# The last FFN of a streaming-encoder block: group 10 with seven block products, x kept in DRAM until the gated sum, and weights in empty slots

## The chip, the cores and the metric

One NeuronCore of a Trainium2 chip. The metric is the device time of one execution in microseconds, the median of several runs.

## The reference, cut to what matters

The input x has 256 tokens of 2048 float32 values. Three sublayers follow one another, each post-normed and modulated by adaLN rows made of the conditioning vector c:

```
mod = silu(c) @ w_ada + b_ada            # shift, scale, gate for each of the sublayers
x = LN1(alpha*x + 1/2*gate0 * SwiGLU_1(mod0(x)))
x = LN2(alpha*x +     gate1 * W_out[ mLSTM(u) || RG-LRU(u) ])     # u = mod1(x)
x = LN3(alpha*x + 1/2*gate2 * SwiGLU_2(mod2(x)))

_swiglu(u, w13, w2): g, v = split(u @ w13);  return (silu(g) * v) @ w2
```

w13 is 2048 x 11264 and w2 is 5632 x 2048, all float32. The change lies in SwiGLU_2 and in what adds its result to x.

## The kernel before, in words

Float32 products are made on TensorE from float32r halves. Each weight tile (128 x 2048, 1 MB) is loaded from DRAM on SP's queue into a raw tile (`load`, L94), ACT casts it into a high half (L108), and DVE subtracts that from the raw tile into a low half (L110). There are four raw buffers and three pairs of halves. The activations are kept as halves too (`uh`, `ul`). A product of a 512 x 512 weight tile with 128 tokens is `mov_t`: 12 matmuls of 512 columns (four slices, each high x high, high x low, low x high); `mov_w` does both token tiles.

The 5632 hidden columns of the last FFN are 11 blocks of 512 columns. A plain block (`rows_block`, L669) loads four g tiles and four v tiles, splits each, and makes 16 products. Blocks 2 to 9 (`FAST`, L46) go through `fast_block` (L711): for the first half of the contraction the four blocks of weights and four of activations are combined as in Strassen's scheme, and 7 products do the work of 8; with the other half 15 are left of 16. The price is four combinations of whole weight tiles on DVE (L756, L761, L766, L775) and three more splits. The combined activations `ws` are made once, by `sums` (L688), and lie in the tile of x; x is stored to DRAM before (L690). In a fast block four w2 tiles of an earlier pair of blocks run between the products (`x_tile`, L733), and their sum is collected in `yacc`, two of six slots. `turn_one` (L803) transposes the gated activations of the block before into the slots `hth`, `htl`, two for each pair of blocks. A tile of a fast block that is used for long lies in one of two row buffers: `ta` always, `tc_` from block 4 on, when the silu(c) row `scb` has left the other.

After block 9 x is loaded back and scaled by alpha (`restore`, L705), the gate row is made (`gate_rows`), and eight `residual` calls (L330) add gate * yacc to x. Block 10 is a plain block. `closing` (L1026) then multiplies the w2 tiles of blocks 8, 9 and 10: nine in a loop for three of the four column groups, and the last group with the gate folded into the weights; `boundary` does the last layer norm and stores.

The adaLN tiles (1 MB each, a multiply and a reduction on DVE, L210) are scattered between the weight loads: each `load` calls `tick`, which adds a rate to a credit and issues a tile (L206) for every whole unit. 16 of these tiles, the gate's, are left for the last FFN; its credit starts at -2 and grows by 0.5. They use the four raw buffers also, and `scb`. They must be done before the gate row.

The order on each engine is planned by the framework's scheduler when the program is built, from the program's order and a model of the durations; instructions of `T`, `A`, `V`, `G`, `Q` keep their program order among themselves. `fast_block` issues its products on `T`.

Of the kernel before, what the change touches and what calls it, by code (L numbers as in the profile page):

```python
# [41 lines left out]
FFN2_RATE = 0.5  # L42
# [3 lines left out]
FAST = range(2, 10)  # L46


class Held:
# [4 lines left out]
    def __getitem__(self, key):  # L54
        return self.tile[key]
# [3 lines left out]
def block_kernel(ctx: ExitStack, tc: tile.TileContext, a: dict, out: bass.AP):  # L59
# [19 lines left out]
    wide = [False]  # L79
    n_raw = [1]  # L80
# [13 lines left out]
    def load(src, name, into=None, raw=None):  # L94

        tick()
        raw = raw or raw_tile("r" + name)
        queue().dma_start(raw, src)
        return raw, name, into
# [554 lines left out]
    def ffn(s, w13, w2, start, following=None):  # L654
# [8 lines left out]
        b0 = RAMP // 4 if start else 0  # L663
# [5 lines left out]
        def rows_block(b, passed=None):  # L669

            i = 8 * (b - b0)
            if passed:
                pg, pv = passed[0], met(passed, w13[4:8], f"fv{s}")
            else:
                pg = [bank(f"fg{s}{b}{t}") for t in range(NT)]
                for k in range(4):
                    end = mov_w(pg, load_w(w13[i + k], f"fg{s}_{b}{k}"), uh, ul, k * 4, k == 0, k == 3)
                    if k in (1, 2):
                        turn_one(end)
                pv = [bank(f"fv{s}{b}{t}") for t in range(NT)]  # L680
                for k in range(4):
                    mov_w(pv, load_w(w13[i + 4 + k], f"fv{s}_{b}{k}"), uh, ul, k * 4, k == 0, k == 3)
            if 4 * b // GRP not in hts:
                new_h(4 * b // GRP)
            for t in range(NT):
                swiglu(b, t, pg[t], pv[t])

        def sums():  # L688

            nc.gpsimd.dma_start(xd, x.tile)  # L690
            f = raw_tile("sums").rearrange("p (a b) -> p a b", b=P)
            for t in range(NT):
                tk = slice(t * P, (t + 1) * P)
                nc.vector.tensor_add(f[:, 8 * t:8 * t + 8, :], uh[:, 0:8, tk].bitcast(F32), ul[:, 0:8, tk].bitcast(F32))
            a11, a12, a21, a22 = (f[:, 4 * i:4 * i + 4, :] for i in range(4))
            nc.vector.tensor_add(a22, a21, a22)
            nc.vector.tensor_sub(a21, a11, a21)
            nc.vector.tensor_sub(a11, a22, a11)
            nc.vector.tensor_sub(a12, a12, a11)
            both = big.tile([P, 2, KT, P], F32R, tag="x", name="ws")  # L700
            nc.scalar.copy(both[:, 0], f)
            nc.vector.tensor_sub(both[:, 1], f, both[:, 0].bitcast(F32))
            return both[:, 0], both[:, 1]

        def restore():  # L705
            x.tile = tokens("x1")
            for t in range(NT):
                nc.gpsimd.dma_start(x[:, t, :], xd[:, t, :])
            scale_x()

        def fast_block(b, wh, wl):  # L711

            i = 8 * b
            gi = 4 * b // GRP - 1
            s2_, s4_, s3_, s1_ = 0, 4, 8, 12
            p1, p5 = bank(f"fa{b}"), bank(f"fb{b}")
            py = {}

            def part(ps, hl, h, k0, t, first, last):
                return mov_t(ps, hl, *h, k0, t, first, last, T, skip_group_check=not first and ps in (p1, p5))  # L720

            def fresh(k, row=False):
                return load(w13[i + k], f"fw{s}_{b}{k}", None, row_tile(f"fw{b}{k}") if row else None)

            def halves(tile, w=""):
                return split((tile[0], tile[1] + w, None), nc.scalar, nc.vector)

            def kept(ps, tag, w):
                to = sm.tile([P, 512], F32, tag=tag, bufs=2, name=f"{w}{s}{b}")
                nc.scalar.copy(to, ps)  # L730
                return to

            def x_tile(m):  # L733
                n, k = b % 2 * 2 + m // 2, m % 2
                if not k:
                    py[n] = [bank(f"py{gi}_{n}_{t}") for t in range(NT)]
                kg = 2 * gi + k
                end = mov_w(py[n], load_w(w2[kg * 4 + n], f"w2{s}_{kg}_{n}"), *hts[gi], k * 4, not k, k == 1, T)
                if k:
                    c = slice(n * 512, (n + 1) * 512)  # L740
                    for t in range(NT):
                        if gi == 0:
                            evac.append(nc.scalar.copy(yacc[t][:, c], py[n][t]))
                        else:
                            nc.vector.tensor_add(yacc[t][:, c], yacc[t][:, c], py[n][t])
                return end

            u, w = (uh, ul), (wh, wl)
            ta = fresh(0, True)
            end = part(p1, halves(ta), u, 0, 0, True, True)  # L750
            turn_one(end)
            f1 = kept(p1, "u", "fs")
            tc_ = fresh(4, b >= 4)
            end = x_tile(0)
            turn_one(end)
            nc.vector.tensor_sub(ta[0], tc_[0], ta[0])  # L756
            part(p5, halves(ta, "p"), w, s1_, 0, True, True)
            f5 = kept(p5, "gy", "ft")
            td = fresh(5)
            x_tile(1)  # L760
            nc.vector.tensor_sub(ta[0], td[0], ta[0])  # L761
            part(p1, halves(ta, "q"), w, s2_, 0, False, True)
            f2 = kept(p1, "gy", "fv")
            part(p5, halves(td), w, s4_, 0, False, False)
            x_tile(2)
            nc.vector.tensor_sub(tc_[0], td[0], tc_[0])  # L766
            part(p1, halves(tc_, "q"), w, s3_, 0, False, True)
            f3 = kept(p1, "u", "fu")
            p2, p4 = bank(f"fc{b}"), bank(f"fd{b}")
            tb = fresh(1)  # L770
            part(p2, halves(tb), u, 4, 0, True, False)
            g2_ = load_w(w13[i + 2], f"fw{s}_{b}2")
            part(p2, g2_, u, 8, 0, False, False)
            part(p4, g2_, u, 8, 1, True, False)
            nc.vector.tensor_sub(tb[0], tb[0], ta[0])  # L775
            part(p4, halves(tb, "p"), u, 4, 1, False, False)
            g3_ = load_w(w13[i + 3], f"fw{s}_{b}3")
            part(p2, g3_, u, 12, 0, False, True)
            part(p4, g3_, u, 12, 1, False, True)
            nc.vector.tensor_add(f1, f1, p2)  # L780
            nc.scalar.activation(f1, f1, AF.Silu)
            nc.vector.tensor_add(f3, f3, p4)
            nc.scalar.activation(f3, f3, AF.Silu)
            x_tile(3)
            vs = [load_w(w13[i + 4 + k], f"fw{s}_{b}{4 + k}") for k in (2, 3)]
            for t, ps in enumerate((p5, p1)):
                for k in range(2):
                    part(ps, vs[k], u, 8 + 4 * k, t, False, k == 1)
            if 4 * b // GRP not in hts:
                new_h(4 * b // GRP)  # L790
            for t, h, v, ps in ((0, f1, f2, p5), (1, f3, f5, p1)):
                nc.vector.tensor_add(v, v, ps)
                nc.vector.tensor_mul(h, h, v)
                to_turn.append((b, t, h))
# [177 lines left out]
        def g1(gi):  # L972
            grp = groups[gi]
            if start and gi == 2:
# [8 lines left out]
            if start and gi == 3:  # L983
# [3 lines left out]
            for b in range(grp[0] // 4, grp[-1] // 4 + 1):  # L987
                if b or start:
                    rows_block(b)
# [36 lines left out]
        def closing(gi):  # L1026

            kgs = [(kg, hts[kg // 2], kg % 2 * 4) for kg in (2 * gi - 2, 2 * gi - 1, 2 * gi)]
            pss, hls = {}, {}

            def gated(k, into=None):

                tile = load(w2[kgs[k][0] * 4 + 3], f"w2{s}l{k}", into)
                for c in range(0, D, 512):
                    nc.vector.tensor_mul(tile[0][:, c:c + 512], tile[0][:, c:c + 512], gate[:, 1536:])
                hls[k] = split(tile, nc.scalar, nc.vector)

            for i, (n, k) in enumerate(((0, 0), (0, 1), (1, 0), (0, 2), (1, 1), (1, 2), (2, 0), (2, 1), (2, 2))):
                kg, h, k0 = kgs[k]
# [519 lines left out]
```

## Time and profile before

| | us |
|---|---|
| median of 3 runs (1881.72 to 1884.14) | 1883.53 |
| the profiled execution | 1882.46 |
| its span, first to last instruction | 1880.7 |
| TensorE busy in the span | 1861.4 (99%) |
| DVE busy | 1561.3 (83%) |
| ACT busy | 895.1 (48%) |
| GpSimd (POOL) busy | 43.2 (2%) |

The span lacks 1.8 us of the execution's own time. In the rows PE is TensorE, PEld its weight load, DVE VectorE, ACT ScalarE, POOL GpSimd, and SP SyncE, which issues most DMAs; a q behind an engine is its queue. Matmuls are pipelined: a row gives each 0.39 us, while the next begins 0.23 us later, so a busy TensorE can still be held up a little. The last FFN begins near 1148 us and its block 2 at 1242.80 us.

### The profile page before, as it was taken

The page shows a single profiled execution, that of the slowest core. Times are in us where ns is not written, and L with a number is a line of the kernel's source. Part 1 is how long each engine was busy: PE and PEld are TensorE (multiplying, and loading weights), DVE is VectorE, ACT ScalarE, POOL GpSimd, SP SyncE. Part 2 cuts the span into 40 slices and gives each one's busy share as a digit, 9 for nine tenths or more (in the row PEclk, how much of TensorE's full clock was granted, in tenths as well). Part 3 has the DMA queues.
Part 4 walks back from the last instruction along what each step waited for, and adds up shares of the span by engine and source line. Part 5 has one row for each costly group of instructions (what it writes and reads, how often), then busy time and mean ns, then how long its engine had stood idle before and what let it go on. Part 6 is the DMA issues. An engine that isn't in the chain of part 4 may idle for free.

```text
span 1880.7 us, 21240 instructions
## 1 busy us (share of the span) xinstructions
PE 1861.4 (99%) x8495; PEld 1526.0 (81%) x8495; DVE 1561.3 (83%) x1467; ACT 895.1 (48%) x847; POOL 43.2 (2%) x68
## 2 busy tenths in 40 slices
PE   8999999999999999999999999999999999999998
PEld 5788888888888888788888887878778888888886
DVE  6899998887887987889997877789887788778776
ACT  4543444533334335756644356454544455545441
POOL 0000000000000000100000121000000000000000
PEclk9999999999999999999999999999999999999999
DMA  9989889999899987478687574768855654564662
GB/s 377 417 354 366 319 311 347 357 348 355 344 357 355 339 331 269 148 276 296 244 317 296 203 264 182 268 246 300 307 210 190 224 212 168 202 224 186 239 224 90
DMA packets 74931, 520.06 MB, mean 277 GB/s; under 512 B 8736, under 2 KB 8912, under 8 KB 13520
## 3 DMA queue, kind: packets, MB, share of 16 engines
q1 hardware_dynamic: 72144, 507.54, 71.6%
q0 software_dynamic: 960, 7.37, 1.0%
q10 hardware_dynamic: 1728, 3.80, 0.6%
q8 instruction: 66, 1.08, 0.2%
q14 instruction: 33, 0.27, 0.0%
HBM read 514.46 MB, written 4.22 MB: 276 GB/s over the span
## 4 chain that ended last, share of the span: by engine, by line
PE 92%; DVE 4%; DMA 2%; issue 1%; ACT 1%; POOL 0%; POOLq 0%; DVEq 0%; SPq 0%; ACTq 0%
PE py L133 9%; PE pj L281 5%; PE fa L133 5%; PE fb L133 4%; PE fc L133 3%; PE fd L133 3%; PE py L293 3%; PE py L294 3%; PE py L292 3%; PE pj L283 3%; PE fg L293 3%; PE fg L294 3%; PE fg L292 3%; PE fv L293 3%; PE fv L292 3%; PE fv L294 3%
## 5 line engine op out<-in xcount | busy, mean ns | idle before, releaser
L210 DVE CUSTOM_DVE_ANT_0 ada<-ada,scb,badac 128x2048 f32<-128x2048 f32 x110 | 258.0, 2345 | 39.5 <-DMA ada<-in_w_ada 39.0
L108 ACT CAST hw<-rw 128x2048 fp32r<-128x2048 f32 x81 | 155.1, 1914 | 218.0 <-DMA rw<-in_w 60.6
L110 DVE TENSOR_TENSOR lw<-rw,hw 128x2048 fp32r<-128x2048 f32 x81 | 185.1, 2287 | 55.8 <-ACT hw L108 55.0
L110 DVE TENSOR_TENSOR lfw<-rfw,hfw 128x2048 fp32r<-128x2048 f32 x48 | 109.9, 2289 | 17.2 <-ACT hfw L108 17.2
L281 PE MATMUL pj<-u,hs 128*128 128x512 f32 x512 | 122.5, 391 | 0.0
L108 ACT CAST hra<-rra 128x2048 fp32r<-128x2048 f32 x38 | 72.6, 1914 | 102.2 <-DMA rra<-in_w_r 43.1
L108 ACT CAST hfw<-rfw 128x2048 fp32r<-128x2048 f32 x48 | 91.9, 1915 | 47.8 <-PE py L133 28.2
L281 PEld LDWEIGHTS pj<-u,hs 128*128 128x128 f32 x512 | 94.3, 188 | 18.4
L133 PE MATMUL py<-lw,hth 128*128 128x512 f32 x256 | 99.8, 390 | 2.1 <-DVE lw L110 2.1
L133 PE MATMUL py<-hw,hth 128*128 128x512 f32 x256 | 100.4, 392 | 0.0
L293 PE MATMUL py<-lw,hth 128*128 128x512 f32 x256 | 99.8, 390 | 0.1
L294 PE MATMUL py<-hw,htl 128*128 128x512 f32 x256 | 99.7, 390 | 0.0
L133 PE MATMUL py<-hw,htl 128*128 128x512 f32 x256 | 99.7, 389 | 0.0
L292 PE MATMUL py<-hw,hth 128*128 128x512 f32 x256 | 97.3, 392 | 0.0
L108 ACT CAST hfg<-rfg 128x2048 fp32r<-128x2048 f32 x28 | 53.6, 1914 | 86.1 <-DMA rfg<-in_w 48.8
L108 ACT CAST hs<-rs 128x2048 fp32r<-128x2048 f32 x32 | 61.0, 1908 | 68.7 <-PE pj L281 53.6
L293 PE MATMUL fg<-lfg,u 128*128 128x512 f32 x224 | 87.4, 390 | 0.1
L294 PE MATMUL fg<-hfg,u 128*128 128x512 f32 x224 | 87.3, 390 | 0.0
L293 PE MATMUL fv<-lfv,u 128*128 128x512 f32 x224 | 87.2, 389 | 0.0
L294 PE MATMUL fv<-hfv,u 128*128 128x512 f32 x224 | 87.1, 389 | 0.0
L108 ACT CAST hfv<-rfv 128x2048 fp32r<-128x2048 f32 x28 | 53.6, 1913 | 66.7 <-DMA rfv<-in_w 41.3
L292 PE MATMUL fg<-hfg,u 128*128 128x512 f32 x224 | 84.5, 392 | 0.0
(727 smaller groups left out, 4764.4 us busy)
## 6 DMA issues: line engine op xcount, KB each, us to landing
ada<-in_w_ada SPq DMA_DIRECT2D x138, 1024.0 KB, 6.5
rw<-in_w SPq DMA_DIRECT2D x81, 1024.0 KB, 5.5
rfw<-in_w SPq DMA_DIRECT2D x50, 1024.0 KB, 4.8
rra<-in_w_r SPq DMA_DIRECT2D x45, 1024.0 KB, 7.4
rs<-in_w_s SPq DMA_DIRECT2D x32, 1024.0 KB, 5.0
rfg<-in_w SPq DMA_DIRECT2D x28, 1024.0 KB, 6.7
rfv<-in_w SPq DMA_DIRECT2D x28, 1024.0 KB, 5.5
rwo<-in_w_out SPq DMA_DIRECT2D x16, 1024.0 KB, 4.8
```

The source lines that it names most:

```text
L108: act.copy(cut(hi, w), like(raw[:, w], hi))
L110: low.tensor_sub(cut(lo, w), like(raw[:, w], lo), cut(hi, w).bitcast(F32))
L133: self.last = getattr(self.engine, op)(*args, **kw)
L210: vec.tensor_tensor_reduce(raw[:, c], raw[:, c], scb[:, c], 1.0, base, ALU.mult, ALU.add, to)
L281: nc.tensor.matmul(ps, hi[:, k * P:(k + 1) * P], both(k), start=k == 0, stop=False)
L283: nc.tensor.matmul(ps[:, 0:S], lo[:, k * P:(k + 1) * P], uh[:, k, :], start=False, stop=k == KT - 1)
L292: pe.matmul(o, acth[:, k0 + j, tk], cut(hi, w), start=first and j == 0, stop=False, **kw)
L293: pe.matmul(o, acth[:, k0 + j, tk], cut(lo, w), start=False, stop=False, **kw)
L294: end = pe.matmul(o, actl[:, k0 + j, tk], cut(hi, w), start=False, stop=last and j == 3, **kw)
```

## The change

`ffn` keeps only the first FFN, and `last_ffn` is new. Constants and helpers:

```diff
-FFN2_RATE = 0.5
+FFN2_RATE = (0.8, 0.3)
-FAST = range(2, 10)
+DOUBLE = ()
+BY_DMA = ()
 class Held:
     def __getitem__(self, key):
+        if isinstance(self.tile, list):
+            p, t, c = key
+            return self.tile[t][p, c]
 def load(src, name, into=None, raw=None):
     tick()
-        raw = raw or raw_tile("r" + name)
+        if raw is None:
+            raw = slot(f"r{name}")[:, 0:D] if extra[0] else raw_tile("r" + name)
```

With `DOUBLE` and `BY_DMA` empty, only one of two halves of the contraction goes by seven products, and no combination is made by a DMA. The scheme's signs are other ones than before; the products and their places stay. A block follows a plan, a list of steps: `t` turns activations of the block before, `X` is one w2 tile, `G` a plain g tile (two products), `V` two plain v tiles (four products), each `P` one product.

```diff
+        S4 = "P1 t X t P5 X P6 P3 X P7 P2 G P4 G X V".split()
+        S2 = "P1 t G t P5 X P6 P3 G P7 P2 X P4 V".split()
...
+                elif w == "P5":
+                    W["c", q] = fresh(q, 4, not DOUBLE and 4 <= b < n_b - 1)
+                    a, c = W["a", q], W["c", q]
+                    vec.tensor_sub(a[0], c[0], a[0])
...
+                elif w == "P6":
+                    d = W["d", q] = fresh(q, 5, q == 1)
+                    vec.scalar_tensor_tensor(a[0], a[0], -1.0, d[0], op0=ALU.mult, op1=ALU.subtract)
...
+                elif w == "P7":
+                        vec.tensor_add(c[0], c[0], d[0])
...
+                elif w == "P4":
+                        vec.tensor_add(a[0], a[0], W["b", q][0])
```

The order of the FFN, and the end:

```diff
+        extra[0] = True
+        credit[:] = 0.0, FFN2_RATE[0]
+        rows_block(0, nxt.pop())
+        scale_x()
+        nc.gpsimd.dma_start(xd, x.tile)
+        rows_block(1)
+        credit[1] = FFN2_RATE[1]
+        ws = [sums(0, in_x)]
+        for b in range(2, n_b - 1, 2):
+            kgs = (b - 2, b - 1)
+            if b == 2:
+                extra[0] = False
+            if b == 4:
+                ada_until(s, 2, KT - 1)
...
+                fast_block(b, ws[:1], x_tiles(kgs, (0, 1)), S4)
+                fast_block(b + 1, ws[:1], x_tiles(kgs, (2, 3)), S4)
+        gate_rows(s, 0.5)
+        for t in range(NT):
+            for n in range(4):
+                c = slice(n * 512, (n + 1) * 512)
+                nc.vector.tensor_mul(yacc[t][:, c], yacc[t][:, c], gate[:, c])
+            nc.gpsimd.dma_start(yacc[t], xd[:, t, :], accum_op=ALU.add)
+        x.tile = yacc
...
+        fast_block(n_b - 1, ws[:1], begun(), S2)
...
+        for i, (n, k) in enumerate(((1, 0), (1, 1), (0, 2), (1, 2), (2, 0), (2, 1), (2, 2))):
```

`begun` gives block 10 the first two w2 tiles of the closing loop, column group 0 of blocks 8 and 9. `turn_one` puts both halves of one block into one slot (`ht`), in place of two slots for each pair. The slots are six as before; loads of blocks 0 and 1 take theirs from the same six while `extra` is set. The rest of the closing loop, the gated w2 tiles and the boundary are as they were, with `yacc` in the place of x.

## Rows read from the trace of the kernel before

**Rows 1.** The page: the span, and the chain that ended last by engine.

```profile
span 1880.7 us, 21240 instructions
...
PE 92%; DVE 4%; DMA 2%; issue 1%; ACT 1%; POOL 0%; POOLq 0%; DVEq 0%; SPq 0%; ACTq 0%
```

**Rows 2.** Busy time by stretch: blocks 0 (part) and 1, 2, 3, 4, 6, 10, closing loop.

```profile
core 0: us, PE busy (x) PEld busy (x) DVE busy (x) ACT busy (x) POOL busy (x), PEclk, DMA share, GB/s
1182.00:1242.80 60.80, 60.80 (x274) 50.31 (x273) 50.32 (x36) 25.22 (x17) 0.00 (x0) 1.00 0.74 278
1242.80:1311.05 68.25, 65.67 (x286) 53.56 (x284) 60.48 (x40) 34.90 (x27) 0.00 (x0) 0.97 0.75 277
1311.05:1376.35 65.30, 64.31 (x286) 52.36 (x284) 56.45 (x37) 34.81 (x27) 0.00 (x0) 1.00 0.76 289
1376.35:1441.82 65.47, 64.15 (x286) 52.68 (x285) 53.82 (x35) 32.76 (x23) 0.00 (x0) 1.00 0.53 194
1505.31:1568.80 63.49, 63.49 (x286) 52.60 (x285) 50.48 (x32) 32.76 (x23) 0.00 (x0) 1.00 0.55 199
1759.44:1804.00 44.56, 44.56 (x202) 36.89 (x202) 32.95 (x31) 19.30 (x14) 0.00 (x0) 1.00 0.54 190
1804.00:1853.00 49.00, 49.00 (x222) 40.59 (x221) 39.01 (x41) 18.35 (x14) 0.00 (x0) 1.00 0.51 192
```

**Rows 3.** The chain that ended last, pieces of block 8: start, us, what.

```profile
1571.53 0.44 PE th L814 x4
...
1586.06 2.72 PE fa L133 x12
```

**Rows 4.** Timeline of TensorE: matmuls with a wait before them, in brackets.

```profile
1263.02 0.50 PE L133 MATMUL fa<-lfw_20q,ws 128*128 128x512 f32 x1 [2.58 <-DVE lfw_20q L110]
...
1381.44 0.50 PE L133 MATMUL py<-lw,hth 128*128 128x512 f32 x1 [1.31 <-DVE lw L110]
```

**Rows 5.** Busy time by stretch, columns as above, behind the first wait.

```profile
1264.00:1268.00 4.00, 4.00 (x12) 3.09 (x12) 3.37 (x2) 0.60 (x2) 0.00 (x0) 0.58 0.66 219
```

**Rows 6.** Timeline of DVE before the first wait and before block 4.

```profile
1258.40 2.35 DVE L210 CUSTOM_DVE_ANT_0 ada<-ada,scb,badac 128x2048 f32<-128x2048 f32 x1 [2.08 <-DMA ada<-in_w_ada]
1260.68 0.08 DVE L210 DVE_READ_ACCUMULATOR2_ANT adac<- 128x1 f32 x1
1260.68 2.29 DVE L110 TENSOR_TENSOR lfw_20q<-fw,hfw_20q 128x2048 fp32r<-128x2048 f32 x1
...
1363.46 2.35 DVE L210 CUSTOM_DVE_ANT_0 ada<-ada,scb,badac 128x2048 f32<-128x2048 f32 x1 [2.17 <-DMA ada<-in_w_ada]
...
1373.49 2.29 DVE L756 TENSOR_TENSOR fw<-fw,fw 128x2048 f32<-128x2048 f32 x1 [3.10 <-DMA fw<-in_w]
```

**Rows 7.** Instructions of the adaLN tiles in the last FFN; then DVE's by stretch.

```profile
L210 DVE CUSTOM_DVE_ANT_0 ada<-ada,scb,badac x16: 2342/2350/2353, 1190.8 to 1363.5; 128x2048 f32<-128x2048 f32 x16
  DMA ada<-in_w_ada: 18.3, 9
...
1182.00:1242.80 60.80, 11.76 (x5) 1.00 0.74 278
1242.80:1311.05 68.25, 14.08 (x6) 0.97 0.75 277
1311.05:1376.35 65.30, 11.74 (x5) 1.00 0.76 289
```

**Rows 8.** DVE's groups by line and shape in block 6: a split, a combination.

```profile
L110 DVE TENSOR_TENSOR lfw<-rfw,hfw 128x2048 fp32r<-128x2048 f32 x6 | 13.7, 2290 | 2.6 <-ACT hfw L108 2.6
...
L756 DVE TENSOR_TENSOR fw<-fw,fw 128x2048 f32<-128x2048 f32 x1 | 2.3, 2291 | 0.0
```

**Rows 9.** Timeline of DVE from the end of block 9 to the end.

```profile
1754.76 0.69 DVE L793 TENSOR_TENSOR fs<-fs,fv 128x512 f32<-128x512 f32 x1
1755.48 0.69 DVE L334 TENSOR_TENSOR gy<-yacc,gate 128x512 f32<-128x512 f32 x1
...
1826.17 0.69 DVE L334 TENSOR_TENSOR gy<-tl,gate 128x512 f32<-128x512 f32 x1 [0.29 <-PE tl L294]
...
1863.74 2.74 DVE L133 SCALAR_TENSOR_TENSOR x<-x,mvp,ln_g 128x512 f32<-128x512 f32 x4
```

**Rows 10.** Timeline of ACT: the scaling; DMA issues: KB, us to landing.

```profile
1745.59 3.71 ACT L133 ACTIVATE x<-x 128x2048 f32<-128x2048 f32 x2
...
xd<-x POOLq DMA_DIRECT2D x1, 2048.0 KB, 11.1
x<-xd POOLq DMA_DIRECT2D x2, 1024.0 KB, 7.4
```

More of the change, by code (lines that the diff above doesn't have):

```diff
@@ L79, in block_kernel @@
     wide = [False]
+    extra = [False]
     n_raw = [1]
@@ L652, in new_stats, with ffn @@
         return [sm.tile([P, 4, 6], F32, tag="sts", bufs=2, name=f"sts{s}{t}") for t in range(NT)]
-    def ffn(s, w13, w2, start, following=None):
+    def ffn(s, w13, w2, start, following):
         yacc = [slot(f"yacc{t}")[:, 0:D] for t in range(NT)]
@@ L662, in ffn @@
         evac = []
-        b0 = RAMP // 4 if start else 0
+        b0 = RAMP // 4
         sts = new_stats(s)
@@ L667, in new_h, with rows_block @@
             hts[gi] = [slot(f"{w}{gi}", F32R)[:, 0:GRP * S].rearrange("p (a b) -> p a b", a=GRP) for w in ("hth", "htl")]
-        def rows_block(b, passed=None):
+        def rows_block(b):
             i = 8 * (b - b0)
[L672 to L682, printed above, removed]
+            pg = [bank(f"fg{s}{b}{t}") for t in range(NT)]
+            for k in range(4):
+                end = mov_w(pg, load_w(w13[i + k], f"fg{s}_{b}{k}"), uh, ul, k * 4, k == 0, k == 3)
+                if k in (1, 2):
+                    turn_one(end)
+            pv = [bank(f"fv{s}{b}{t}") for t in range(NT)]
+            for k in range(4):
+                mov_w(pv, load_w(w13[i + 4 + k], f"fv{s}_{b}{k}"), uh, ul, k * 4, k == 0, k == 3)
             if 4 * b // GRP not in hts:
@@ L686, in rows_block @@
                 swiglu(b, t, pg[t], pv[t])
[L688 to L794, printed above, removed]
@@ L973, in g1 @@
             grp = groups[gi]
-            if start and gi == 2:
+            if gi == 2:
                 new_h(gi)
@@ L982, in g1 @@
                 return
-            if start and gi == 3:
+            if gi == 3:
                 for t in range(NT):
@@ L987, in g1 @@
             for b in range(grp[0] // 4, grp[-1] // 4 + 1):
-                if b or start:
-                    rows_block(b)
+                rows_block(b)
         def g2(gi):
@@ L1024, in g2_kept @@
                         turn_one(end)
[L1026 to L1039, printed above, removed]
-                if not k:
-                    pss[n] = [bank(f"tl{s}{t}{n}") for t in range(NT)]
-                end = mov_w(pss[n], load_w(w2[kg * 4 + n], f"w2{s}_{kg}_{n}"), *h, k0, not k, k == 2)
-                if i:
-                    turn_one(end)
-                if i in (2, 5):
-                    gated(i // 2, half(i // 5))
-                if k == 2:
-                    for t in range(NT):
-                        residual(s, t, n, pss[n][t], sts, nc.vector)
-            credit[:] = 0.0, 0.0
-            fine[0] = True
-            gated(0)
-            def last(ps, t, n):
-                for i, (_, h, k0) in enumerate(kgs):
-                    end = mov_t(ps, hls[i], *h, k0, t, i == 0, i == 2)
-                return end
-            boundary(s, {}, hls, ((3,), (3,)), last, sts, None, True)
-        done = 0
-        if start is not None:
-            ramp(start)
-            credit[:] = 0.0, FFN1_RATE
-            done = 2
-            g2(0)
-        else:
-            credit[:] = -2.0, FFN2_RATE
-            rows_block(0, nxt.pop())
-            rows_block(1)
-            ws = sums()
-            for b in FAST:
-                fast_block(b, *ws)
-            restore()
-            done = FAST.stop // 2 - 1
-        for gi in range(done, len(groups)):
-            if start or gi > done:
-                g1(gi)
+        ramp(start)
+        credit[:] = 0.0, FFN1_RATE
+        g2(0)
+        for gi in range(2, len(groups)):
+            g1(gi)
             if gi == len(groups) - 2:
@@ L1083, in ffn @@
                 credit[0] -= 2.0
-            if gi == len(groups) - 1 and following:
+            if gi == len(groups) - 1:
                 credit[:] = 0.0, 0.0
                 g2_kept(gi - 1)
-            elif gi == len(groups) - 1:
-                closing(gi)
-            elif gi:
-                if start:
-                    g2(gi - 1)
+            else:
+                g2(gi - 1)
                 if gi == len(groups) - 2:
@@ L1095, in ffn @@
                             residual(s, t, n, yacc[t][:, n * 512:(n + 1) * 512], None)
-        if not following:
-            return
         ada_until(s + 1, 1, KT - 1)
@@ L1466, in block_kernel @@
     mixer((a["w13_2"][0:8], "f", (0, 1), (1,), (), True, 6))
[L1467 removed]
+    last_ffn(2, a["w13_2"], a["w2_2"])
 def _ada_tiles():
```

214 lines of the change are left out of this document (213 added, 1 removed).

## The prediction

> **What bounds the kernel now.** I read the page first: the span, and the chain that ended last, which is TensorE for 92% of its time [rows 1]. DVE, DMA and issue make up 7% of it, so the question is where TensorE waits. The second view is the busy time by stretch, cut at the blocks of the last FFN [rows 2]. A block here is one of the 11 groups of 512 hidden columns, and the diff calls them groups. From block 5 on a block lasts 63.49 us and TensorE is busy for all of it. One product (12 matmuls of 512 columns) takes 2.72 us on the chain and a turn of the gated activations 0.44 us [rows 3]. A fast block has 15 products for w13, 8 for four w2 tiles and two turns: 23 x 2.72 + 2 x 0.44 = 63.4 us. The long run from block 5 on is therefore pure TensorE work.
>
> Blocks 2, 3 and 4 are longer: 68.25, 65.30 and 65.47 us [rows 2]. Against 63.49 they lose 4.76 + 1.81 + 1.98 = 8.55 us. This is the only slack there is in the last FFN. The timeline of TensorE shows it as waits for a low half that DVE writes [rows 4]; behind the longest (2.58 us) the granted clock in the next 4 us is 0.58, so part of the time ran at the 1.2 GHz level before it was back at 2.4 GHz [rows 5]. DVE's own timeline says why DVE was late [rows 6]: before the first wait it stood 2.08 us for an adaLN tile from DRAM, worked 2.35 us on it, and only then made the low half. By block 4 it stood 3.10 us for a weight tile: tile c of block 4 takes the second row buffer, which the last adaLN tile releases. 16 such tiles fall into the last FFN; nine of them kept DVE waiting, 18.3 us in all [rows 7]. Counting their rows by start, five ran before block 2, six in block 2, five in block 3.
>
> **The change, part by part.**
>
> *Block 10 by seven products.* rows_block spends 16 products; the S2 plan spends 15. One product goes: -2.72 us [rows 3]. Its two w2 tiles are moved ahead from the closing loop, with their loads on SP's queue, and keep their price. What is added lies on DVE: splits rise from 8 to 11, and four full-size combinations come in. With the two w2 tiles block 10 has 13 low halves and 4 combinations of 2.29 us [rows 8] = 38.9 us, eight gating multiplies of 0.69 us = 5.5 us and eight small operations of the same size = 5.5 us [rows 9], together 49.9 us. TensorE has 19 products and two turns there, 52.6 us. The cover is thin but whole on average. The old row of this block shows DVE busy 32.95 of 44.56 us. S2's demanding middle (P6, P3, two products, P7, P2, two products, P4) is in order that of the fast blocks, which run without a wait. Bounds: 0 to 14.7 us (the combinations and the gating multiplies all uncovered, 9.2 + 5.5); I take +1.0, near the lower end, because the fast blocks are the nearest row.
>
> *The closing loop* shrinks from nine w2 tiles to seven. Its old row has DVE at 39.0 of 49.0 us [rows 2]; less two splits it is 34.4 us against 7 x 5.44 + 0.9 = 39.0 us. I take 0, bound 0 to +2.7 (one product's time).
>
> *x kept in DRAM, scaled first, added by an accumulating DMA.* Two scalings of x (3.71 us in all) move on ACT from the end of block 9 into blocks 0 and 1 [rows 10]; ACT is busy 25.22 of 60.80 us in most of that stretch [rows 2]. If the scheduler put them before the last casts of the boundary they could cost 3.7 us; I take 0. The store of x now waits on POOL's queue for that scaling and is issued after block 0; the boundary's last small operations on POOL come before it, and behind it stands nothing until the gate rows. It took 11.1 us to land [rows 10], and its reader is the buffer of the combined activations, needed by the second product of block 2, some 50 us later. At the end eight additions leave DVE (8 x 0.69 = 5.5 us), which is inside the count above. The two loads become accumulating ones of 1 MB each. No row has an accumulating DMA: the nearest is the plain reload, median 7.4 us. Its first reader is the residual that stood at 1826.17 us [rows 9], over 55 us after the gating. Even three times 7.4 us for each of two in a row is hidden. Bound: 0 to +1, through contention; below nothing is excluded since nothing waits for the old reload. Taken: 0.
>
> *One slot per block for the turned activations, in place of two per pair of blocks.* Two halves in one slot, same bytes, same writers: 0.
>
> *Signs.* Three subtractions become additions or keep their form: 0. One becomes a scalar_tensor_tensor over two f32 tiles in SBUF. The tail has that operation at 128x512: four take 2.74 us, 0.69 each, and a tensor multiply of the same size takes 0.69 us too [rows 9]. So I take 2.29 us at full size. The Trainium skill ("Vector Engine (DVE) Microarchitecture Reference", section "Points that are easy to get wrong") says that this form with two non-bf16 SBUF sources halves throughput; by it the operation would cost 4.58 us, and the sum would lose what the last rival gives. The rows do not agree with it.
>
> *Slots for the weights of blocks 0 and 1; adaLN rates 0.8, then 0.3.* TensorE is busy 60.80 of 60.80 us before block 2, so quicker weight loads there gain nothing by themselves. What they give is the four raw buffers to adaLN tiles, and DVE has 10.5 us idle in that stretch [rows 2]. Old credits: 11 loads, -2 + 5.5, three tiles and two more through SP running ahead. New: 11 x 0.8 = 8.8, eight tiles and one ahead. So seven tiles instead of 11 remain for blocks 2 and 3; four leave, 4 x 2.35 = 9.4 us of DVE time and some of the 18.3 us of waits [rows 7]. Gain there: by proportion 4/11 of 6.57 = 2.4 us; at most all 8.55 us. Waits of a queue near its limit shrink faster than its load, so I take 4.5 us. Block 4's 1.98 us I leave: the 16th tile still ends block 3 (8.8 + 24 x 0.3 = 16.0), and tile c still waits for it.
>
> **Sum:** -2.72 + 1.0 - 4.5 = -6.2 us. The profiled execution took 1882.46 us, so it would be 1876.2; the median of the runs is 1883.53, 1.07 above. I predict 1877.3 us for the median, -0.33%. A measurement of this kernel can tell about 0.2%, 3.8 us, from no change.
>
> **The rivals.**
>
> *All of the slack comes back.* -2.72 - 8.55 = -11.3 us, 1872.3 us. For it: DVE idles 13.0 us in an even block [rows 2], and seven tiles need 16.5 us over two. Against: block 4's wait for the row buffer. Chance 0.14.
>
> *The relief does not come.* adaLN loads still stand behind weights in SP's queue, or the scheduler places them in blocks 2 and 3 anyway, and block 10 costs 1 us: -1.7 us, 1881.8 us; the slots would then not do what they are there for. For it: what delays DVE is the landing of an adaLN tile, not only their number, and block 2 lost 4.76 us with DVE at only 60.5 of 68.25 us. Chance 0.20, within 0.2%.
>
> *DVE becomes the bound in block 10.* It would be 95% busy there, more than in block 2 with 89%. With three pairs of split buffers, and c back in a raw buffer since the gate holds a row buffer, combinations and gating multiplies could stand uncovered between products: up to 14.7 us. -2.72 - 4.5 + 14.7 = +7.5 us, 1891.0 us. It decides from 7.2 us of uncovered DVE work, three full-size operations. Against: DVE idles while V's four products of block 9 run. Chance 0.10, slower.
>
> *The reversed subtraction is slow.* At 4.58 us it takes back 2.29 us in each of blocks 2 and 3, half of the relief, and 2.29 us more in block 10: -2.72 + 1.0 - 2.3 + 2.3 = -1.7 us, 1881.8 us. The equal 0.69 us speak against it. Chance 0.04, within 0.2%. This is the operation of which the page cited above speaks.
>
> **The numbers.** The forecast has 0.52; it and the first rival are faster by over 0.2%: 0.66. The second and the fourth give 0.24 for within 0.2%; the third 0.10 for slower. The range goes from 1872.0, just under the full recovery, to 1884.5, which takes in the relief that does not come with its bounds of +2.7 us for the tail; above lie the slow rival and a few in a hundred more.
>
> **What would show it.** Right: block 10 has TensorE busy throughout about 52.6 us; nine adaLN tiles before block 2; blocks 2 and 3 together 2 us or less over 127.0; block 4 still about 65.5; the reversed subtraction at 2.3 us; the accumulating DMA landed long before the first residual. Wrong: waits of TensorE for low halves in block 10 or in the closing loop, a clock below 1.0 there, a wait for weights in block 0, or blocks 2 and 3 as long as before.

## The result, and the profile after

| | before | after |
|---|---|---|
| median, 6 runs each, us | 1883.84 | 1890.53 (1887.6 to 1891.49) |
| ratio, 95% interval | | 1.0033 [1.002, 1.0046] |
| the profiled execution, us | 1882.46 | 1887.6 |
| its span, us | 1880.7 | 1885.8 |

The change makes the kernel slower by 0.33%; the forecast was faster by 0.33%, and 1890.53 lies above its range. The page of the kernel after gives the span and the shares of the chain that ended last; they answer to [rows 1].

```profile
span 1885.8 us, 21245 instructions
...
PE 89%; DVE 5%; DMA 2%; ACT 2%; issue 2%; POOL 0%; POOLq 0%; DVEq 0%; SPq 0%; ACTq 0%
```

TensorE's share of the chain fell from 92% to 89%: it waits more. To see where, I cut both spans at one instruction that both kernels have, the first transpose of a block's turn (the turn of the block before it). A turn is named by the block in which it runs. The numbers are us; the spans are known to 0.1 us. The traced execution after is the fastest of its six: the two traces differ by 5.1 us, the medians by 6.7.

| stretch | before | after | difference |
|---|---|---|---|
| start of span to block 1's first turn | 1209.23 | 1212.80 | +3.57 |
| block 1's to block 2's | 36.29 | 46.94 | +10.65 |
| block 2's to block 9's (seven blocks) | 452.83 | 444.45 | -8.38 |
| block 9's to the end of the span | 182.35 | 181.61 | -0.74 |
| sum, the difference of the spans | | | +5.1 |

So the relief of blocks 2 to 4 came, and in this cut it is nearly twice the forecast: 7 x 63.49 = 444.43 us is what seven undisturbed blocks take, and 444.45 is what they take now. The loss of 14.22 us lies ahead of them, in blocks 0 and 1, to which the prediction gave nothing. The busy time by stretch of the kernel after, with the columns of [rows 2]: first blocks 0 (part) and 1, a part of block 1 and the 10 us behind its waits, then blocks 2, 3, 4, 10 and the closing loop.

```profile
1182.00:1257.18 75.18, 64.44 (x277) 52.20 (x276) 60.43 (x42) 28.55 (x19) 0.65 (x1) 0.93 0.65 255
1199.46:1220.00 20.54, 14.04 (x65) 11.45 (x63) 17.42 (x17) 4.44 (x4) 0.00 (x0) 0.90 0.70 272
1220.00:1230.00 10.00, 8.49 (x29) 6.40 (x30) 6.97 (x4) 3.99 (x3) 0.00 (x0) 0.70 1.01 422
1257.18:1320.51 63.33, 63.33 (x284) 52.44 (x284) 52.95 (x34) 34.90 (x27) 0.00 (x0) 1.00 0.68 249
1320.51:1384.01 63.50, 63.50 (x286) 52.60 (x285) 54.44 (x34) 34.93 (x27) 0.00 (x0) 1.00 0.69 265
1384.01:1447.50 63.49, 63.49 (x286) 52.60 (x284) 50.47 (x32) 32.88 (x23) 0.00 (x0) 1.00 0.55 199
1765.13:1819.92 54.79, 53.65 (x238) 43.51 (x237) 46.97 (x32) 31.08 (x22) 0.00 (x0) 1.00 0.64 215
1819.92:1859.00 39.08, 39.08 (x178) 32.34 (x177) 35.30 (x40) 14.54 (x12) 0.00 (x0) 1.00 0.48 187
```

The first row is the one to read: 75.18 us, and TensorE busy for 64.44, where before it was busy for all of its 60.80 us [rows 2]. The longest waits of TensorE in the whole span (us in total, times, longest) say on what:

```profile
PE fg L298 <- ACT hfg L114: 6.5, 1, 6.5
PE f L299 <- DVE lfv2b L116: 2.7, 1, 2.7
...
PE fg L299 <- DVE lfg L116: 1.5, 1, 1.5
```

In order of time: 2.74 us in block 0, for a low half (`lfv2b`) that DVE makes after an adaLN tile; then, in block 1, 6.50 us for the cast of its third g tile and 1.50 us for the low half of the same. The waits of block 1 add to 8.0 us of its 10.65; behind them the granted clock is 0.70 over 10 us, so a part of these ran at the 1.2 GHz level. The kernel before has 1.00 there. Who held up the third tile? The timeline of ACT around it:

```profile
1213.44 0.59 ACT L975 CAST ht<-th 128x512 fp32r<-128x512 f32 x1 [14.84 <-PE th L973]
1216.15 1.90 ACT L1007 CAST ws<-sums 128x2048 fp32r<-128x2048 f32 x1 [2.13 <-DVE sums L1005]
1217.95 3.69 ACT L114 CAST hfg<-rfg 128x2048 fp32r<-128x2048 f32 x2
```

ACT stands 14.84 us for the first turn (its transposes are queued on TensorE behind two g tiles), then 2.13 us for DVE's sums, and only then casts the tile for which TensorE stands. The casts come in the order of the plan; both items ahead of them are for later products. In the kernel before, ACT casts the third g tile well ahead of the turn:

```profile
1198.54 1.92 ACT L108 CAST hfg<-rfg 128x2048 fp32r<-128x2048 f32 x1 [3.52 <-PE fv2b L294]
...
1211.24 0.57 ACT L816 CAST hth<-th 128x512 fp32r<-128x512 f32 x1
```

And the tile was not there either. SP's timeline, in which a row is an issue or several of one kind merged, and SP's waits from 1200 to 1212 us:

```profile
1174.92 22.51 SPq L212 DMA_DIRECT2D ada<-in_w_ada  x6
1201.58 0.33 SPq L104 DMA_DIRECT2D rw<-in_w  x1
1209.53 0.33 SPq L104 DMA_DIRECT2D rfw<-in_w  x1
1209.95 0.86 SPq L104 DMA_DIRECT2D rfg<-in_w  x2
1210.90 1.75 SPq L104 DMA_DIRECT2D rfv<-in_w  x3
...
SPq L104 <- DVE adac L216: 11.6, 2, 7.5
```

`rw` and `rfw` are tiles of block 2: they go into raw buffers that adaLN tiles still hold, and SP waits 11.6 us in two pieces until DVE has released these. Behind them in the same queue stand five loads of block 1, two `rfg` and three `rfv`, which leave at 1209.95 us and later. So a plan that put block 2's loads ahead of block 1's made block 1 wait for the adaLN tiles. The third g tile took 6.8 us to land, to about 1216.8, so here ACT's order cost only the last 1.2 us; it becomes the limit once SP's order is mended (f1 below). In the kernel before, the same tiles leave early:

```profile
1186.65 6.85 SPq L98 DMA_DIRECT2D rfg<-in_w  x2
...
1197.58 6.21 SPq L98 DMA_DIRECT2D rfv<-in_w  x2
```

The adaLN tiles themselves, with the rows that answer to [rows 7]: their form, DVE's waits for them, and (columns of [rows 2]) their DVE time in the stretches before block 2, in block 2 and in block 3.

```profile
L216 DVE CUSTOM_DVE_ANT_0 ada<-ada,scb,badac x16: 2342/2351/2355, 1164.3 to 1360.0; 128x2048 f32<-128x2048 f32 x16
  DMA ada<-in_w_ada: 1.5, 1
...
1150.00:1257.18 107.18, 0.00 (x0) 0.00 (x0) 23.43 (x10) 0.95 0.71 284
1257.18:1320.51 63.33, 0.00 (x0) 0.00 (x0) 7.04 (x3) 1.00 0.68 249
1320.51:1384.01 63.50, 0.00 (x0) 0.00 (x0) 7.05 (x3) 1.00 0.69 265
```

Ten, three and three, where it was five, six and five; DVE waits 1.5 us for them in all, where it was 18.3. Of the rest of the change, the rows of DVE for the reversed subtraction and the gating, the DMAs (KB each, us from issue to landing) that answer to [rows 10], and TensorE's two waits in block 10:

```profile
1261.54 2.29 DVE L1104 SCALAR_TENSOR_TENSOR fw<-fw,rfw 128x2048 f32<-128x2048 f32 x1
...
1755.62 4.91 DVE L1191 TENSOR_TENSOR yacc<-yacc,gate 128x512 f32<-128x512 f32 x8 [0.50 <-DMA gate<-rowd]
...
xd<-x POOLq DMA_DIRECT2D x1, 2048.0 KB, 12.1
yacc<-xd POOLq DMA_DIRECT2D x2, 1024.0 KB, 9.9
...
1783.32 0.50 PE L139 MATMUL f<-lfw_100q,ws 128*128 128x512 f32 x1 [0.24 <-DVE lfw_100q L116]
1789.93 0.50 PE L139 MATMUL f<-lfw,u 128*128 128x512 f32 x1 [0.83 <-DVE lfw L116]
```

### The profile page after: what moved, and what is told of

Same layout as the page of the kernel before. It is cut to its first block, busy times and chain, and to the rows that moved or that the text cites. A ratio compares the mean times of both kernels' runs of the same rounds, so it can differ in the third digit from the quotient of the medians.

```text
span 1885.8 us, 21245 instructions
## 1 busy us (share of the span) xinstructions
PE 1860.1 (99%) x8483; PEld 1525.3 (81%) x8483; DVE 1573.0 (83%) x1470; ACT 902.9 (48%) x854; POOL 43.7 (2%) x68
## 4 chain that ended last, share of the span: by engine, by line
PE 89%; DVE 5%; DMA 2%; ACT 2%; issue 2%; POOL 0%; POOLq 0%; DVEq 0%; SPq 0%; ACTq 0%
PE f L139 18%; PE py L139 9%; PE pj L287 5%; PE py L299 3%; PE py L298 3%; PE py L300 3%; PE pj L289 3%; PE fg L299 2%; PE fg L300 2%; PE fv L298 2%; PE fg L298 2%; PE fv L299 2%; PE fv L300 2%; PE tl L299 2%; PE tl L298 2%; PE tl L300 2%
## 5 line engine op out<-in xcount | busy, mean ns | idle before, releaser
L139 PE MATMUL f<-hfw,u 128*128 128x512 f32 x720 | 226.5, 389 | 0.0
L139 PE MATMUL py<-hw,ht 128*128 128x512 f32 x512 | 163.7, 391 | 0.0
L139 PEld LDWEIGHTS f<-hfw,u 128*128 128x128 f32 x720 | 135.2, 188 | 28.0
L139 PE MATMUL f<-lfw,u 128*128 128x512 f32 x360 | 140.1, 389 | 0.8 <-DVE lfw L116 0.8
L139 PEld LDWEIGHTS py<-hw,ht 128*128 128x128 f32 x512 | 96.1, 188 | 19.8
L299 PE MATMUL py<-lw,hth 128*128 128x512 f32 x256 | 99.8, 390 | 0.1
L300 PE MATMUL py<-hw,htl 128*128 128x512 f32 x256 | 99.7, 390 | 0.0
L139 PE MATMUL py<-lw,ht 128*128 128x512 f32 x256 | 99.6, 389 | 0.0
L298 PE MATMUL py<-hw,hth 128*128 128x512 f32 x256 | 97.3, 392 | 0.0
L298 PE MATMUL fg<-hfg,u 128*128 128x512 f32 x192 | 72.5, 397 | 6.5 <-ACT hfg L114 6.5
```

The costliest lines, as they stand in the source:

```text
L139: self.last = getattr(self.engine, op)(*args, **kw)
L298: pe.matmul(o, acth[:, k0 + j, tk], cut(hi, w), start=first and j == 0, stop=False, **kw)
L299: pe.matmul(o, acth[:, k0 + j, tk], cut(lo, w), start=False, stop=False, **kw)
L300: end = pe.matmul(o, actl[:, k0 + j, tk], cut(hi, w), start=False, stop=last and j == 3, **kw)
```

## The experiments

The theory after the result: the wait in blocks 0 and 1 comes from the slots and the order that is planned for them (rival first: the burst of adaLN tiles ahead of block 2). Each diff is against the kernel after and shows the lines that matter; g1 and g2 contain f5's edit too, g2 also those of g1 and e3, and `cast[0]` is the last weight cast on ACT. The medians of the kernel before, beside the runs, were 1882.35 us (first four), 1883.12 (next four), 1884.3 (next three) and 1883.18 (last); as they move by up to 2 us, the ratios to them, with their 95% intervals, are what runs of different groups are compared by. "Turn of block 2" is the first of its two, as in the table above: 1245.52 us before and 1259.74 us after. Where an expectation says that block 2 starts, it means the product ahead of that turn: 1242.80 us before and 1257.18 us after.

**Old rate of adaLN tiles, slots kept** (e1).

```diff
-FFN2_RATE = (0.8, 0.3)
+FFN2_RATE = (0.5, 0.5)
-        credit[:] = 0.0, FFN2_RATE[0]
+        credit[:] = -2.0, FFN2_RATE[0]
```

> The changed kernel with the old adaLN credit (starts at -2, grows by 0.5 throughout); slots, plans and the end stay. In the changed kernel block 2 starts at 1257.2 us instead of 1242.8. Theory (a burst of adaLN tiles holds the raw buffers and stands in SP's queue before the weights of block 1): block 2 starts at 1243 to 1246 again, blocks 2 to 4 lose 4 to 8.6 us again, and the profiled time is 1877 to 1882 us. Rival (the slots themselves: the scheduler orders block 1's loads badly when they come from slots): block 2 still starts after 1252 us and the time stays at 1888 us or more.

1894.85 us, ratio 1.0068 [1.0053, 1.0083]. The turn of block 2 stands at 1260.81 us, TensorE still waits 4.2 us for `hfg` and 4.0 us for `lfv2b`, and the waits of block 3 are back (its turn to block 4's: 67.72 us). Six adaLN tiles ahead of block 2 in place of ten mend nothing there: the burst theory falls.

**No slots, new rates** (e2).

```diff
-        extra[0] = True
+        extra[0] = False
```

> The changed kernel without the loads into slots; rates 0.8 and 0.3 stay. Theory (the burst): weights and adaLN tiles now share four raw buffers in blocks 0 and 1, so block 2 still starts after 1252 us and the time is 1885 to 1895 us. Rival (the slots): block 2 starts at 1243 to 1247 us and the time is 1874 to 1878 us.

1879.83 us, 0.9986 [0.9976, 0.9995]: 10.7 us less than the kernel after by the medians, 0.47% (8.9 us) by the ratios, as between the two spans. Turn of block 2 at 1247.44 us, its start one product ahead: as the rival had it, with the time just past the rival's bounds. Block 2 pays some of it, 67.55 us from its turn to block 3's, with waits of 1.1 us for `ws` and 1.1 and 0.9 us for low halves; later blocks take 63.5. So the slots cost about 12 us ahead of block 2 and gave about 4 in it.

**Gating multiplies after the first of block 10's two w2 tiles** (e3).

```diff
-        for t in range(NT):
-            ...
+        def gated_sum():
+            ...
             for k in range(2):
+                if k:
+                    gated_sum()
                 yield yx_tile(kgs, 0, k, pss[0], not k, False)
```

> The changed kernel with the eight gating multiplies and the accumulating DMAs issued before the second w2 tile of block 10 instead of before block 10. Theory (in block 10 TensorE loses 2.2 us because DVE stands for the gate row and then does 4.9 us of gating in a row): blocks 10 and closing take 2 us less, 107.9 instead of 110.1 us, the time is 2 us below the changed kernel. Rival (DVE is short of time in S2 in any order): no difference, within 0.5 us.

1890.16 us, 1.0036 [1.0021, 1.005], as the kernel after. From block 10's first turn to the closing loop's it takes 56.84 us, after 57.35. The 0.5 us is no case for the gating as what uncovers block 10: with the gating where the change has it, e1 takes 56.95 and e2 56.77 us. This trace also tells how far one execution can be trusted: ahead of block 10 its program is that of the kernel after, its waits in blocks 0 and 1 are the same 2.7, 6.5 and 1.5 us, and yet its turn of block 2 stands at 1262.85 us, 3.1 later. The granted clock is 0.57 from 1186 to 1190 us and 0.52 from 1220 to 1230, where the kernel after has 0.70.

**The scaling of x left out** (e4; alpha is then missing from the last sublayer's residual).

```diff
         rows_block(0, nxt.pop())
-        scale_x()
```

> The changed kernel without the scaling of x by alpha in the last sublayer (that step is left out, so x enters the sum unscaled). Theory (the burst): ACT's 3.7 us and the later store of x are covered; block 2 starts within 2 us of 1257.2 us. Rival (ACT's order and the late store of x delay the combined activations and the casts behind them): block 2 starts before 1250 us and the time falls by over 6 us.

1884.67 us, one execution. Turn of block 2 at 1257.17 us, 2.6 earlier; the 2.7 us wait for `lfv2b` is gone, that for `hfg` is there with 7.1 us. With the scaling gone most of block 0's loss is gone too (block 1's first turn at 1210.26 us, 1.0 behind the kernel before), block 1's is not; g1 below tells whether it is the scaling's place on ACT.

**SP in program order through blocks 0 to 3, all slots** (f1).

```diff
-        return Q if wide[0] else nc.sync
+        return Q if wide[0] or in_order[0] else nc.sync
...
-        extra[0] = True
+        extra[0] = in_order[0] = True
...
             if b == 4:
+                in_order[0] = False
```

> The changed kernel with SP's loads of blocks 0 to 3 kept in program order; slots and rates stay. The first turn of block 2 began at 1259.7 us in the changed kernel, 1247.4 without slots, 1245.5 in the kernel before. Theory (five weight loads of block 1 stand in SP's queue behind two loads of block 2, which wait for raw buffers that adaLN tiles hold): the first turn of block 2 comes before 1250 us, the time is 1881 us or less. Rival (the slots themselves come free late, in whatever order SP issues): it comes after 1257 us and the time is 1887 us or more.

1885.37 us, 1.0013 [1.0003, 1.0022], turn of block 2 at 1254.71: 5.0 of the 14.2 us are back, between the two expectations. ACT's timeline shows what holds up block 1 now:

```profile
1211.17 0.59 ACT L976 CAST ht<-th 128x512 fp32r<-128x512 f32 x1 [14.85 <-PE th L974]
1211.65 3.70 ACT L115 CAST hfg<-rfg 128x2048 fp32r<-128x2048 f32 x2
```

The load of the third g tile leaves by 1183.96 us now, not at 1209.95, but ACT still idles 14.85 us for the turn with the cast queued behind it. TensorE's waits in this run:

```profile
PE fg L299 <- ACT hfg L115: 2.5, 1, 2.5
...
PE fg L300 <- DVE lfg L117: 1.1, 1, 1.1
```

**adaLN tiles in slots, weights in raw buffers** (f4).

```diff
-            raw = slot(f"r{name}")[:, 0:D] if extra[0] else raw_tile("r" + name)
+            raw = raw_tile("r" + name)
...
-        raw = raw_tile(f"ada{i}") if raw is None else raw
+        if raw is None:
+            raw = slot(f"ada{i}")[:, 0:D] if extra[0] else raw_tile(f"ada{i}")
```

> The changed kernel with the roles exchanged: in blocks 0 and 1 the adaLN tiles are loaded into slots and the weights into the four raw buffers. Theory (what hurts is the order of weights in SP's queue): all weights share one kind of buffer, stay in order, the first turn of block 2 comes before 1249 us and the time is 1874 to 1880 us. Rival (nine adaLN tiles before block 2 are too many for DVE): it comes after 1252 us, the time is 1884 us or more.

1883.95 us, 1.0003 [0.9994, 1.0012]. The turn of block 2 is at 1249.70 us, with a wait of 1.4 us for `lfv2b` in block 0, but block 2 takes 69.17, with waits of 1.8 and 1.5 us. No gain.

**Only the first five loads in slots** (f5).

```diff
             raw = slot(f"r{name}")[:, 0:D] if extra[0] else raw_tile("r" + name)
+            n_slot[0] += extra[0]
+            if n_slot[0] == 5:
+                extra[0] = False
```

> The changed kernel with slots for the first five weight loads only, the other six of blocks 0 and 1 in raw buffers; rates stay. In the planned order no load of block 2 is then ahead of one of block 1. Theory (the order): the first turn of block 2 comes before 1249 us, the time is 1875 to 1881 us. Rival (any slot load: adaLN tiles get raw buffers early and delay DVE at the boundary, where TensorE waited 2.7 us): it comes after 1252 us.

1879.38 us, 0.9976 [0.9966, 0.9985]: faster than both kernels. Turn of block 2 at 1249.30 us, a little later than expected, and block 2 takes 64.12. ACT now casts the third g tile at 1202.32 us, before the turn's evacuation at 1215.02. The 2.7 us wait in block 0 is still there.

**Block 10 by 16 products, no slots** (f6), against e2.

```diff
-        fast_block(n_b - 1, ws[:1], begun(), S2)
+        rows_block(n_b - 1)
...
-        for i, (n, k) in enumerate(((1, 0), (1, 1), (0, 2), (1, 2), (2, 0), (2, 1), (2, 2))):
+        for i, (n, k) in enumerate(((0, 0), (0, 1), (1, 0), (0, 2), (1, 1), (1, 2), (2, 0), (2, 1), (2, 2))):
...
```

The places of the turns and of the gated tiles in the loop go back to those of before as well.

> The changed kernel without slots, and with block 10 as a plain block of 16 products and nine w2 tiles in the closing loop, as before. Beside the run without slots (1879.83 us) it prices the product. Theory (2.72 us saved, about 1.5 us lost in block 10 to late low halves): 0.8 to 1.8 us slower than the run without slots, about 1881.1 us. Rival (the seven products of block 10 cost what they save): within 0.5 us of 1879.8 us.

1880.28 us, 0.9987 [0.9978, 0.9996]. From block 9's turn to the end: 182.35 us, with the seven products (e2) 180.95. So the part of the change in block 10 is worth about 1.4 us in these traces; the medians, 0.45 us apart, can't tell it.

**Five slots, the scaling of x queued behind block 0's last cast** (g1).

```diff
...
-        scale_x()
+        with tc.issue_after(cast[0].ins):
+            scale_x()
```

> Five slot loads as in the run before, and the two scalings of x queued on ACT behind the last cast of block 0. In the five-slot run ACT did them (3.7 us) between the second and the third cast of block 0. Theory (the scaling in that place delays a low half that TensorE waits for; leaving it out took 2.6 us off the first turn of block 2): first turn of block 2 at 1246 to 1247.5 us instead of 1249.3, time 1876.5 to 1878 us instead of 1879.4. Rival (two adaLN tiles on DVE delay that low half as much, so ACT's order is hidden): first turn within 0.7 us of 1249.3, time within 0.7 us of 1879.4.

1879.38 us, 0.9977 [0.9968, 0.9985], as f5. Turn of block 2 at 1250.66 us, and the `lfv2b` wait is still 2.8 us. The scaling's place on ACT is not what sets it. The 1.4 us by which the turn is later than in f5 go with the clock: 0.61 granted from 1186 to 1190 us, where f5 has 1.00 behind the same wait. What goes with the wait is DVE's order: in the kernel after, adaLN tiles at 1176.61 and 1181.29 us stand ahead of the first low half `lfv2b`, and so they do in f5, g1 and g2 within 0.3 us of these times, each with a wait of 2.7 or 2.8 us.

```profile
1181.29 2.35 DVE L216 CUSTOM_DVE_ANT_0 ada<-ada,scb,badac 128x2048 f32<-128x2048 f32 x1
...
1183.56 4.49 DVE L116 TENSOR_TENSOR lfv2b<-rfv2b,hfv2b 128x2048 fp32r<-128x2048 f32 x2
```

In e2, e4 and h2 (below), all without the wait, no adaLN tile runs between 1175 us and that low half, and the next one runs behind it. The low half begins at 1180.36 us in e2, at 1180.39 in e4, and in h2 as here:

```profile
1181.12 4.49 DVE L120 TENSOR_TENSOR lfv2b<-rfv2b,hfv2b 128x2048 fp32r<-128x2048 f32 x2
1185.52 2.35 DVE L220 CUSTOM_DVE_ANT_0 ada<-ada,scb,badac 128x2048 f32<-128x2048 f32 x1
```

No run pins DVE's order by itself, so this stays a reading of the traces.

**The same, later gating, and fewer adaLN tiles ahead of block 2** (g2).

```diff
-FFN2_RATE = (0.8, 0.3)
+FFN2_RATE = (0.8, 0.38)
-        credit[:] = 0.0, FFN2_RATE[0]
+        credit[:] = -1.6, FFN2_RATE[0]
...
```

> As the run with the later scaling, with the credit starting at -1.6 and rates 0.8 and 0.38 (about two adaLN tiles fewer before block 2), and the gating multiplies in the middle of block 10. Theory (adaLN tiles at the boundary are the rest of the delay in block 0, and DVE bears 0.38 in blocks 2 and 3): first turn of block 2 at 1245 to 1246.5 us, blocks 2 and 3 within 1 us of 63.5 us each, time 1875 to 1876.5 us. Rival (two more tiles in blocks 2 and 3 bring the waits back): blocks 2 and 3 over 66 us, time above the run with the later scaling alone.

1885.08 us, 1.0006 [0.9998, 1.0015]. The turn of block 2 at 1250.83 us, and blocks 2 and 3 at 66.27 and 66.95 us: the tiles moved back into them bring their waits back. With eight tiles ahead of block 2 in place of ten the `lfv2b` wait is still 2.7 us, so the theory fails on block 0 too.

**SP in program order, and each turn's evacuation behind the next weight cast; all slots** (g3; f1 with this).

```diff
+                    if k == 1:
+                        hl.update((j, load_w(w13[i + j], f"fg{s}_{b}{j}")) for j in (1, 2))
...
-                        turn_one(end)
+                        with tc.issue_after(cast[0].ins):
+                            turn_one(end)
...
```

The loads and splits of the second and third g tile are also written ahead of the second one's products, so that there is a next cast to queue the turn behind.

> All eleven slot loads, SP in program order as in the run before with that order (1885.4 us, first turn of block 2 at 1254.7 us), and in addition each turn's evacuation on ACT queued behind the cast of the next weight tile. In that run and in the changed kernel ACT has the first turn's evacuation ahead of the cast of block 1's third tile, though the tile had long landed. Theory (the planned order on ACT is the second half of the loss): first turn of block 2 before 1252 us, time 1882.5 us or less. Rival (DVE's adaLN tiles are the rest of the loss): first turn after 1254 us, time within 1 us of 1885.4.

1879.88 us, 0.9979 [0.997, 0.9987], turn of block 2 at 1250.18 us: 10.6 us less than the kernel after, with every slot as the change has it. ACT's timeline of this run:

```profile
1200.36 1.92 ACT L116 CAST hfg<-rfg 128x2048 fp32r<-128x2048 f32 x1 [3.98 <-PE fv2b L302]
1211.22 0.59 ACT L977 CAST ht<-th 128x512 fp32r<-128x512 f32 x1 [8.95 <-PE th L975]
1211.70 1.92 ACT L116 CAST hfg<-rfg 128x2048 fp32r<-128x2048 f32 x1
```

The cast leaves before the turn, at 1200.36 us and not behind it at 1211.65 as in f1; TensorE's waits on `hfg` are gone, as the theory had it. With the orders of SP and ACT pinned, eleven slots cost nothing that the medians show against none (1879.88 and 1879.83 us), though the turn of block 2 is 2.7 us later than in e2. So it was not the slots as memory but the order in the two queues that made most of the loss. ACT's order alone was not pinned in any run. That the tile "had long landed", as the expectation has it, holds for f1 and not for the kernel after, where it landed at about 1216.8 us, behind the turn's evacuation.

**Two slots, for the first two loads of block 1** (h2).

```diff
-        extra[0] = True
         rows_block(0, nxt.pop())
+        extra[0] = True
...
+            if n_slot[0] == 2:
+                extra[0] = False
```

> The changed kernel with two loads into slots, the first two of block 1; block 0 loads into raw buffers as before. In the planned order no load of block 2 stands before one of block 1 on SP, and the casts of block 1's third and fourth tile stand before the first turn's evacuation on ACT. Theory (early slot loads let two adaLN tiles onto DVE at the boundary, and a good order is all that the rest needs): first turn of block 2 before 1247 us, block 2 under 65 us, time 1875.5 to 1878.5 us. Rival (DVE loses the same with any place for the adaLN tiles): first turn after 1248.5 us, time 1879 us or more.

1878.74 us, 0.9974 [0.9965, 0.9984], the lowest median of the study, 0.26% under the kernel before. Turn of block 2 at 1247.15 us and no `lfv2b` wait, but block 2 takes 67.25 us and not under 65, with 1.8 us for one low half, and a granted clock of 0.57 from 1264 to 1268 us behind it:

```profile
PE f L143 <- DVE lfw_20q L120: 1.8, 1, 1.8
```

The intervals of h2, f5, g1, g3 and e2 overlap: two, five, eleven well ordered or no slots at all come out within 1.2 us of one another (1878.74 to 1879.88 us).

## Why the prediction was wrong

**The step that failed is the one on the slots**: "quicker weight loads there gain nothing by themselves", with no cost beside it. It asked only what the slots give, and took TensorE's 60.80 busy of 60.80 us as a state that stays. That stretch was full because loads and casts came in a good order, and the change draws up a new one: loads of three kinds (slots, raw buffers, adaLN tiles) share SP's one queue, and here two loads whose buffers weren't free stood 11.6 us ahead of five that block 1 needed. In place of the 0 stands +14.22 us. Undoing the slots (e2) takes back 12.3 us of it, pinning SP's order (f1) 5.0, and pinning ACT's order too (g3) 9.6, at the same number of slots. The prediction named "a wait for weights in block 0" as a sign of wrong, but as a sign with no price; the rival for the slower side was put into block 10. A change that rearranges the buffers of a full stretch needed a rival there: the two loads stood 4.1 and 7.5 us for the release of an adaLN tile's buffer, and everything behind them as long.

**Relief in blocks 2 to 4**: the mechanism was right. Taken -4.5 us, measured -8.38 between the turns, all the slack, as the first rival had it. Two parts of the working were off: ten adaLN tiles came before block 2, not nine, and DVE's waits for them fell from 18.3 to 1.5 us, more than in proportion. Block 4's 1.98 us, which the prediction left in place, went too: the last adaLN tile ran at 1360.0 us, well before block 4 at 1384.01, and block 4 took 63.49 us. Part of that may be a gift of the loss ahead, since adaLN tiles land while TensorE stands; e2, with 1.9 us of the loss left, recovers 4.3 of the 8.38 us, and g3, with all slots and 4.7 us of it, 6.6 (446.2 us from block 2's turn to block 9's). It does not go by the loss alone: f5, with 3.8 us of it, recovers 7.75 (445.08 us), f4, with 4.2, only 2.7. Up to block 9's turn, loss and relief together, e2 is 2.4, h2 3.0 and f5 4.0 us ahead of the kernel before (1695.95, 1695.36 and 1694.38 us against 1698.35): with a good order the -4.5 is nearly there, and not more.

**Block 10**: -2.72 + 1.0 = -1.7 us was predicted; the traces show -0.74 in the kernel after and about -1.4 between f6 and e2, the same sign and less than the size. It took 54.79 us, not 52.6, with TensorE busy 53.65; two waits of 0.24 and 0.83 us for low halves are the uncovered part that rows show. Later gating (e3) brought back nothing that runs without it lack. What the rest is made of stays open.

**What held**: the closing loop kept TensorE busy for 39.08 of 39.08 us, as counted. The accumulating DMAs took 9.9 us each, more than the 7.4 of the plain reload [rows 10], and were hidden, as was the store of x. The reversed subtraction took 2.29 us, as the 0.69 us rows of the tail had it [rows 9]; the rule of the Trainium skill that was weighed ("Vector Engine (DVE) Microarchitecture Reference", section "Points that are easy to get wrong"), by which it would be an estimated 4.58 us, is not borne out here. The sum of the rival on it was wrong besides: 2.29 us in each of blocks 2 and 3 are 4.58, the whole relief and not half, so it would have given +0.6 us, not -1.7.

**What stays open.** Why the plan puts block 2's loads ahead of block 1's, and ACT's evacuation ahead of the cast, is not shown: it is drawn up when the kernel is built, and the trace shows only its outcome. Leaving the scaling out (e4) removed block 0's wait of 2.7 us, moving it (g1) did not. The plan of the kernel after has the scaling ahead of block 0's last cast, the case that the prediction bounded by 3.7 us and took at 0; by g1 its place is worth nothing, and the adaLN tiles ahead of the low half are the nearest cause that the traces offer. And no run has both the early turn of block 2 (1247.15 us in h2) and the short blocks 2 to 8 (444.45 us after); together with the end of e2 they would give about 1247.15 + 444.45 + 180.95 = 1872.6 us of span, an estimate from these rows, 4.4 us under h2's 1877.0; whether one plan can have all three is not shown.

## What to carry to other kernels

Spare buffers given to loads are not free when the order of issue is planned: a new kind of buffer changes which load waits for which release. On SP's queue here, two early loads that couldn't start held up five that block 1 needed. Before costing such a step at nothing, list per queue (the loading queue and the casting engine) what will stand ahead of the next tile that TensorE needs; where a plan is not in your hand, pin the order or give out fewer buffers (two, five and none did better than eleven in the planned order, and no better than eleven in a pinned one). And cut both traces at an instruction that both have: a net of +5.1 us was +14.2 and -9.1.

## What the runs showed of the hardware beyond expectation

A wait of TensorE can cost more than itself, and not by the same each time. Behind the 6.50 and 1.50 us of block 1 the granted clock was 0.70 from 1220 to 1230 us, where the same stretch of the kernel before was at 1.00, and block 1 lost 10.65 us, 2.65 more than the waits; behind the same waits e3 had 0.52 and lost 11.95. Behind a wait of 2.8 us g1 had 0.61 over 4 us, f5 behind its 2.7 us 1.00, and g1's next turn came 1.4 us later. An accumulating DMA of 1 MB from DRAM into SBUF landed in 9.9 us in the kernel after, a third more than the plain load of the same size and queue in the kernel before (7.4). A scalar_tensor_tensor over two float32 tiles in SBUF cost what a plain subtraction does, 2.29 us at 128x2048.
